# Moving column sums and a folding to other places in TensorE's queue, in a one-core convolution block

## The chip, the core and the metric

The kernel runs on one core of a Trainium2 chip. The metric is the device time of one execution in microseconds (us); lower is better. The engines are called as in the profile: PE (TensorE's matmuls), PEld (its weight loads), DVE (VectorE), ACT (ScalarE), POOL (GpSimd), SP (SyncE, which here issues nearly all DMAs). Each engine works through its own queue in order, and an instruction that must wait for another engine holds up everything behind it in its queue.

## The reference

One layer of a decoder with a convolution mixer, for 256 tokens of width 2048, all in float32. Cut to what is computed:

```python
mod = silu(c) @ mod_w + mod_b                 # 6 vectors of 2048: sh1, sc1, g1, sh2, sc2, g2
h = rms_norm(x, norm1_g) * (1 + sc1) + sh1
a, gt = split(h @ conv_w_in + conv_b_in)      # 2048 x 4096
u = a * sigmoid(gt)
u = depthwise_conv(u, 31 taps, causal) + dw_b # each of 2048 channels for itself
u = silu(layer_norm(u, ln_g, ln_b))           # mean and variance over the 2048 channels
x = x + (1 + g1) * (u @ conv_w_out + conv_b_out)
h = rms_norm(x, norm2_g) * (1 + sc2) + sh2
x = x + (1 + g2) * (square(relu(h @ mlp_w1)) @ mlp_w2)
```

## The kernel before

Channels lie on partitions: the width is cut into 16 tiles of 128 channels, each 128x256 (channels by tokens). A float32 product is made of reduced-precision parts: ACT writes the upper part `hi` of a weight tile (L209), DVE or POOL the rest `lo` (L213), and `mm` issues hi times hi, hi times lo and lo times hi.

The work on PE is a list of jobs, in order: 16 jobs "in" (job n gives tile n of `a` and of the gate), 8 jobs "out", and then the MLP's "up" and "down". The first eight "in" jobs are computed together at the start. The change lies in the jobs "in" 8 to 15, which stand between 136 and 291 us of the span. After the matmuls of job n (L238 and L239, for job 15 L234 to L236) its result is evacuated and gated: ACT L536, DVE L537, ACT L817 (sigmoid), DVE L819, which writes `u[n]`, the input of the convolution of tile n.

The convolution is shared out. Tiles 2, 3, 4, 5, 6, 8, 11 and 13 are done on DVE, one instruction per tap (L670, L672, L674, L676) and a joining sum (L679); `advance(n)` issues the next n of these steps, and the table `ADVANCE` says how many after each job. Tile 7 is shared by ACT and POOL. Tiles 0, 1, 9, 10, 12, 14 and 15 are done on PE (`pe_conv`, L802): `copy_wide` copies `u` into four shifted pieces (16 copies on ACT at L779, for tile 15 eight of them on DVE at L777), POOL writes the taps as diagonals (L787), and PE multiplies in strips of 32 columns. `CONV_AT` says after which job each such tile's convolution stands.

The layer norm needs sums of the convolved tiles and of their squares over all channels. For precision a shift is subtracted first: `find_shift` sums tiles 0 and 1 over their channels (two full-width matmuls, L428) into the PSUM tile `small`, and ACT writes the negative mean into the other half of `small` and into `shift` in SBUF (L737). From tile 8 on, DVE's second tap adds the shift from `small` (L674); `add_shift` (L741) and POOL (L908) add it to the others. `stats(b)` squares tiles 4b to 4b+3 on ACT (L480) and sums tiles and squares over channels with matmuls in strips of 32 columns (L747), again into `small`; `fold_stats` and `add_stats` finish.

The modulation vectors come in two ways. Rows (`mod_chunk`, L328) are matmuls in strips of 32 columns with weights that arrive by DMA, spread over the jobs; every 16 chunks, `mod_finish` folds the collected row into columns with small full-width matmuls (L375), from which DVE adds the bias (L366). Columns (`mod_col`, L408) are one DVE instruction of 128x2048 each; one of them is taken in job 15.

The order within each engine's queue is set by a planner that simulates the program when it is built. `tc.issue_after(x)` keeps what follows behind instruction x in that order, `urgent()` raises a priority; what has neither may be moved to where the planner sees room. The framework adds the waits that the data needs: a matmul that writes a tile waits for the engines that, by the order in which the code is written, read this tile before.

Two lines that the text below speaks of, the tap that reads `small` and the shift of tile 12 ahead of the column of job 15:

```python
            nc.vector.scalar_tensor_tensor(out, s, w, state["small"][:, T : 2 * T], op0=ALU.mult, op1=ALU.add)   # L674
                state["e_end"] = add_shift(cvs[3][:, 0:1, :], 1)                                                 # L915
        with tc.issue_after(state["e_end"]) if "e_end" in state else ExitStack():                                # L407
```

Of the kernel before, what the change touches and what calls it, by code (L numbers as in the profile page):

```python
# [11 lines left out]
ALU = mybir.AluOpType  # L12
# [5 lines left out]
KT = D // P  # L18
# [25 lines left out]
CONV_AT = {9: (0,), 10: (1,), 11: (9,), 12: (10,), 14: (12,), 15: (14,)}  # L44
POOL_TILE = 7
POOL_TAPS = {8: 2, 9: 7, 10: 7, 11: 7, 12: 7}
ADVANCE = {7: 41, 8: 10, 9: 44, 10: 47, 11: 39, 12: 34, 13: 24, 14: 99}
SHIFT = 2
COPY_AT = {8: 0, 9: 1, 10: 9, 11: 10, 13: 12}
PADDING = 752  # L50
UNSHIFTED = 7
# [17 lines left out]
def conv_block(ctx: ExitStack, tc: tile.TileContext, x, vec, dwq, c_row, mod_r, mod_c, w_first, w_in, w_out, w1, w2, out):  # L69
    nc = tc.nc  # L70
# [30 lines left out]
    ones = const.tile([P, P], F32, name="ones")  # L101
# [18 lines left out]
    state = {"used": 0}  # L120
# [247 lines left out]
    def mod_finish():  # L368
        while pending:
            ats, nj, r = pending.pop(0)  # L370
            n = len(ats)
            p = ps.tile([P, 512], F32, name="row", bufs=1)
            with urgent():
                for j in range(nj):
                    state["fold_end"] = nc.tensor.matmul(  # L375
                        p[:, n * j : n * j + n], r[:, j * P : (j + 1) * P], col("pick", 0, n), start=True, stop=True
                    )
                for b, at in enumerate(ats):
                    with tc.issue_after(state["lo_end"]) if "lo_end" in state else ExitStack():
                        mod_bias(at, nj, p[:, 0 : nj * n].rearrange("p (j n) -> p n j", n=n)[:, b, :])  # L380
# [16 lines left out]
    def mod_col(at, w=None):  # L397
        w = (take(("col", at)) if w is None else w).rearrange("p k n -> p (k n)")
        which, k = divmod(at, KT)
        acc = modc[:, at : at + 1]  # L400
        if which == SH2 and "cond" in state:
            n = HALF * P
            for half, total in zip(state["cond"], (acc, rest2[:, k : k + 1])):
                nc.vector.scalar_tensor_tensor(w[:, 0:n], w[:, 0:n], 1.0, half, op0=ALU.mult, op1=ALU.mult, accum_out=total)
                w = w[:, n:]
            return
        with tc.issue_after(state["e_end"]) if "e_end" in state else ExitStack():  # L407
            nc.vector.scalar_tensor_tensor(w, w, 1.0, cb, op0=ALU.mult, op1=ALU.mult, accum_out=acc)  # L408
        if which in amps:
            return nc.vector.scalar_tensor_tensor(  # L410
                amps[which][:, k : k + 1], acc, col("modb", at), col("n1g", k), op0=ALU.add, op1=ALU.mult
            )
        elif which != SH2:
            return mod_bias(at, 1, acc)
# [10 lines left out]

    def column_sum(p, tiles, first=True, last=True):
        for i, s in enumerate(tiles):
            nc.tensor.matmul(  # L428
                p, ones, s, start=first and i == 0, stop=last and i == len(tiles) - 1
            )  # L430

    def inverse_root(ms, src, scale, r, then=None):
        w = two()
# [109 lines left out]
    for k2 in range(HALF):  # L543
        s = two()
# [111 lines left out]
    def cv(k):  # L656
        return cvs[k // 4][:, k % 4, :]
# [73 lines left out]
    def find_shift():  # L731
        state["small"] = ps.tile([P, 512], F32, name="small", bufs=1)
        p = state["small"][:, 0:T]
        column_sum(p, [cv(k) for k in range(SHIFT)])
        state["shift"] = cp.tile([P, T], F32, name="shift", bufs=1)
        for dst in (state["small"][:, T : 2 * T], state["shift"]):
            nc.scalar.activation(dst, p, AF.Copy, scale=-1.0 / (SHIFT * P))  # L737

    def add_shift(tiles, n):
        by = state["small"][:, None, T : 2 * T].to_broadcast([P, n, T])  # L740
        return nc.vector.tensor_tensor(tiles, tiles, by, op=ALU.add).ins  # L741
# [9 lines left out]
    def stats(b):  # L751
        s = squares(cvs[b])
        for k in range(2):
            sum_round([(cv(4 * b + 2 * m + k), s[:, 2 * m + k, :]) for m in range(2)], b == 0 and k == 0)
# [15 lines left out]
    def copy_wide(ct, both=True):  # L770
        wides[ct] = cp.tile([P, 4, T + 28], F32, name="wide", bufs=2)
        for q in range(4):
            for g in range(4):
                dst = wides[ct][32 * q : 32 * q + 32, g, :]
                src = u[ct][32 * g : 32 * g + 32, q : q + T + 28]
                if both and g % 2:
                    nc.vector.tensor_copy(dst, src)  # L777
                else:
                    nc.scalar.activation(dst, src, AF.Copy)  # L779
# [14 lines left out]
    def pe_conv(ct, sq=None):  # L794
        wide = wides.pop(ct)
        diag = diags.pop(ct)
        p = ps.tile([P, 2, 2 * T], F32, name="mm", bufs=2)[:, 0, 0:T] if sq is None else ps_two()[:, 0, :]
        if sq is not None:
            nc.tensor.matmul(p, col("ident", 0, P), state["shift"], start=True, stop=False)
        for m in range(8):  # L800
            for g in range(4):
                state["conv_end"] = nc.tensor.matmul(  # L802
                    p[32 * g : 32 * g + 32, :], diag[:, 8 * g + m, :], wide[:, g, 4 * m : 4 * m + T],
                    start=(m == 0 and sq is None), stop=(m == 7),
                )
        with urgent():
            if ct == 14:
                nc.vector.scalar_tensor_tensor(cv(ct), p, col("dwb", ct), state["shift"], op0=ALU.add, op1=ALU.add)
            elif sq is None:
                nc.scalar.activation(cv(ct), p, AF.Identity, bias=col("dwb", ct))  # L810
            else:
                nc.vector.tensor_scalar(cv(ct), p, col("dwb", ct), None, op0=ALU.add)
                nc.scalar.activation(sq, p, AF.Square, bias=col("dwb", ct))
# [8 lines left out]
        return sg  # L822

    def mix(ct):
        pe_conv(ct)
        if ct == SHIFT - 1:
            find_shift()

    with urgent():
        split_w(jobs[HELD] + (0,), nc.gpsimd)  # L830
# [12 lines left out]
    for n, job in enumerate(jobs):  # L843
# [52 lines left out]
        else:  # L896
            for c in range(2):
                mm(p, c, job + (c,), hl, merged=kind == "out")
        mod_finish()
        if kind == "in":  # L900
            with urgent():
                gate(i, evac(p, out=p[:, :, 0:T]) if i < KT - 1 else p[:, :, 0:T])
# [9 lines left out]
            if n == KT - 2:  # L912
                add_shift(cvs[2][:, 1:3, :], 2)
            if n == KT - 1:
                state["e_end"] = add_shift(cvs[3][:, 0:1, :], 1)  # L915
                for key, w in taken:
                    mod_col(key[1], w)
            for ct in CONV_AT.get(n, ()):
                with tc.issue_after(state["mm_end"].ins):
                    mix(ct)  # L920
                with tc.issue_after(state["conv_end"].ins):
                    mods(rows)
                if rows:
                    state["rows_end"] = state["row_end"].ins
            if rows:
                mod_finish()
            with tc.issue_after(state["gated"]):
                advance(ADVANCE.get(n, 0))
            if n == KT - 2:
                with tc.issue_after(state["mm_end"].ins):  # L930
                    for b in range(2):
                        stats(b)
            if n < KT - 1:
                continue
            sq15 = two()
# [244 lines left out]
```

## Time and profile before

| what | us |
|---|---|
| median of 3 runs (1095.54 to 1095.91) | 1095.86 |
| the profiled execution | 1095.74 |
| its span | 1093.8 |
| PE busy in the span | 1075.9 (98%) |
| DVE busy | 748.5 (68%) |
| ACT busy | 520.1 (48%) |
| POOL busy | 217.4 (20%) |

In a row of a timeline stand the start, the length, the engine, the kernel's line, the operation, output and inputs with their shape, and how many instructions are merged in it; behind it in brackets how long the engine was idle before, and what ended that. One float32 matmul is two instructions of PE in the trace, so a group of 8 is 4 matmuls. In a table of windows, PEclk is the granted share of PE's clock.

### The profile page before, as it was taken

How to read it: one execution, taken by the hardware profiler on the slowest of the kernel's cores; microseconds unless marked ns; L12 is line 12 of the kernel's file. 1: busy time of each engine (PE TensorE's matmuls, PEld its weight loads, DVE VectorE, ACT ScalarE, POOL GpSimd, SP SyncE). 2: the span in 40 equal slices, each digit the busy share in tenths (PEclk: the TensorE clock that was granted, in tenths of full speed). 3: DMA queues.
4: the chain of work that ended last, by engine and by line, in shares of the span. 5: the costliest groups of instructions: out<-in, count | busy, mean ns of one | idle time of the engine just before them, and what ended most of it. 6: DMA issues, size and time to landing. Idle time of an engine off the chain costs nothing.

```text
span 1093.8 us, 15366 instructions
## 1 busy us (share of the span) xinstructions
PE 1075.9 (98%) x5970; PEld 889.9 (81%) x5970; DVE 748.5 (68%) x1019; ACT 520.1 (48%) x706; POOL 217.4 (20%) x149
## 2 busy tenths in 40 slices
PE   6999999999999999999999999999999999999998
PEld 3877876768699988888888888888888888888887
DVE  5777889997667877768855677545566665565653
ACT  4111398677675686444444444333444333444431
POOL 0000169989599251000000000000000000000000
PEclk8999999999999999999999999999999999999999
DMA  9999997995999967899977889657888877788611
GB/s 384 420 420 420 416 416 288 391 371 216 375 393 403 372 248 253 265 296 341 419 266 206 253 258 318 235 144 290 248 242 237 225 214 214 230 251 235 214 66 39
DMA packets 142314, 314.20 MB, mean 287 GB/s; under 512 B 87585, under 2 KB 105505, under 8 KB 107297
## 3 DMA queue, kind: packets, MB, share of 16 engines
q1 hardware_dynamic: 142096, 313.10, 81.6%
q8 instruction: 47, 0.77, 0.3%
q14 instruction: 25, 0.20, 0.0%
q10 hardware_dynamic: 146, 0.13, 0.0%
HBM read 301.13 MB, written 12.07 MB: 286 GB/s over the span
## 4 chain that ended last, share of the span: by engine, by line
PE 86%; DMA 10%; DVE 3%; ACT 1%; issue 0%; SPq 0%; ACTq 0%
PE mm L276 20%; PE mm L275 20%; PE mm L277 20%; DMA raw<-mod_c 9%; PE mm L238 6%; PE mm L239 3%; PE acc L235 2%; PE acc L234 2%; PE acc L236 2%; PE row L328 2%; PE mm L802 2%; DVE raw L408 1%; DMA x<-x 1%; DVE wide L777 1%; PE mm L234 0%; PE mm L236 0%
## 5 line engine op out<-in xcount | busy, mean ns | idle before, releaser
L209 ACT ACTIVATE hi<-raw 128x1024 fp32r<-128x1024 f32 x320 | 335.7, 1058 | 357.4 <-PE mm L277 328.3
L213 DVE TENSOR_TENSOR lo<-raw,hi 128x1024 fp32r<-128x1024 f32 x257 | 312.3, 1220 | 182.7 <-ACT hi L209 180.9
L276 PE MATMUL mm<-lo,u 128*128 128x512 f32 x496 | 193.0, 389 | 0.0
L275 PE MATMUL mm<-hi,u 128*128 128x512 f32 x496 | 193.0, 389 | 0.0
L277 PE MATMUL mm<-hi,u 128*128 128x512 f32 x496 | 192.9, 389 | 0.0
L277 PE MATMUL mm<-hi,hl 128*128 128x512 f32 x480 | 186.7, 389 | 0.0
L276 PE MATMUL mm<-lo,hl 128*128 128x512 f32 x480 | 186.7, 389 | 0.0
L275 PE MATMUL mm<-hi,hl 128*128 128x512 f32 x480 | 186.7, 389 | 0.0
L213 POOL TENSOR_TENSOR lo<-raw,hi 128x1024 fp32r<-128x1024 f32 x63 | 156.2, 2506 | 33.4 <-ACT hi L209 33.3
L408 DVE SCALAR_TENSOR_TENSOR raw<-raw,cond 128x2048 f32<-128x2048 f32 x50 | 117.8, 2358 | 40.5 <-DMA raw<-mod_c 40.5
L277 PEld LDWEIGHTS mm<-hi,u 128*128 128x128 f32 x496 | 93.1, 188 | 19.3
L276 PEld LDWEIGHTS mm<-lo,u 128*128 128x128 f32 x496 | 93.1, 188 | 19.1
L275 PEld LDWEIGHTS mm<-hi,u 128*128 128x128 f32 x496 | 93.1, 188 | 19.0
L277 PEld LDWEIGHTS mm<-hi,hl 128*128 128x128 f32 x480 | 90.1, 188 | 18.7
L275 PEld LDWEIGHTS mm<-hi,hl 128*128 128x128 f32 x480 | 90.1, 188 | 18.7
L276 PEld LDWEIGHTS mm<-lo,hl 128*128 128x128 f32 x480 | 90.1, 188 | 18.7
L676 DVE SCALAR_TENSOR_TENSOR acc<-u,v,acc 128x256 f32<-128x256 f32 x224 | 95.8, 488 | 1.8
L238 PE MATMUL mm<-hl,hi 128*128 128x512 f32 x224 | 80.3, 402 | 0.0
L580 PE MATMUL mm<-two,first 128*128 128x256 f32 x240 | 56.7, 390 | 8.9 <-ACT two L638 8.9
L234 PE MATMUL acc<-hl,hi 128*128 128x256 f32 x224 | 63.4, 283 | 0.0
L235 PE MATMUL acc<-hl,hi 128*128 128x256 f32 x224 | 63.4, 283 | 0.0
L236 PE MATMUL acc<-hl,lo 128*128 128x256 f32 x224 | 63.4, 283 | 0.0
(218 smaller groups left out, 1286.8 us busy)
## 6 DMA issues: line engine op xcount, KB each, us to landing
raw<-w SPq DMA_DIRECT2D x128, 1024.0 KB, 5.5
raw<-mod_c SPq DMA_DIRECT2D x62, 1024.0 KB, 11.3
raw<-mod_r SPq DMA_DIRECT2D x32, 1024.0 KB, 8.7
raw<-w_in SPq DMA_DIRECT2D x16, 1024.0 KB, 11.2
raw<-w_out SPq DMA_DIRECT2D x16, 1024.0 KB, 7.9
first<-w_first SPq DMA_DIRECT2D x15, 1024.0 KB, 19.8
flat<-two SPq DMA_DIRECT2D x30, 256.0 KB, 2.6
two<-flat SPq DMA_DIRECT2D x120, 64.0 KB, 4.4
```

The source lines that it names most:

```text
L209: state["w_hi"] = nc.scalar.activation(hi, w[:, ks, :], AF.Copy).ins
L213: end = by.tensor_tensor(lo, w[:, ks, :], hi.bitcast(F32), op=ALU.subtract)
L234: nc.tensor.matmul(out_p, w, m[:, 0:T], start=begin, stop=False)
L235: nc.tensor.matmul(out_p, w, m[:, T : 2 * T], start=False, stop=False)
L236: state["mm_end"] = nc.tensor.matmul(out_p, lo[:, k % HALF, :], m[:, 0:T], start=False, stop=end)
L238: nc.tensor.matmul(p[:, c, :], hi[:, k % HALF, :], m, start=(k == 0), stop=(k == KT - 1))
L275: nc.tensor.matmul(p, p_hi, hi, start=begin, stop=False)
L276: nc.tensor.matmul(p, p_hi, lo, start=False, stop=False)
L277: nc.tensor.matmul(p, p_lo, hi, start=False, stop=end)
L408: nc.vector.scalar_tensor_tensor(w, w, 1.0, cb, op0=ALU.mult, op1=ALU.mult, accum_out=acc)
L580: step = nc.tensor.matmul(held[n][:, c, :], w[:, 2 * n + c, :], h, start=k == 0 and c == 0, stop=k == KT - 1, skip_group_check=True)
L676: nc.vector.scalar_tensor_tensor(out, s, w, acc, op0=ALU.mult, op1=ALU.add)
```

## The change

- `find_shift` is issued ahead of the convolution of tile 9 (after job 11), and no longer behind that of tile 1 (after job 10). So that no tap reads the shift before it is there, `ADVANCE` gives job 10 five steps fewer and job 11 five more; five steps of job 13 go to job 14.
- `mod_finish`, the folding, is issued right behind the last matmul of its job, ahead of the convolution of that job; the later call behind the rows is dropped.
- `stats(0)` is issued in job 13 behind its rows, `stats(1)` in job 14 behind the convolution of tile 12; before, both were issued in job 14 behind its matmuls. The next job's matmuls are kept behind them.
- In job 15, the shift of tile 12 reads `shift` in SBUF, no longer `small`, and is written behind the column that job 15 takes, no longer ahead of it. `state["e_end"]` is set there, so that the column (L407) has no instruction to stand behind.
- The copies of tile 15 go ten to ACT and six to DVE, no longer eight and eight.

```diff
-ADVANCE = {7: 41, 8: 10, 9: 44, 10: 47, 11: 39, 12: 34, 13: 24, 14: 99}
+ADVANCE = {7: 41, 8: 10, 9: 44, 10: 42, 11: 44, 12: 34, 13: 19, 14: 99}
+SHIFT_AT = 9
...
     def find_shift():
...
-        column_sum(p, [cv(k) for k in range(SHIFT)])
+        end = column_sum(p, [cv(k) for k in range(SHIFT)])
...
+        return end
...
-                if both and g % 2:
+                if both and g % 2 and q:
                     nc.vector.tensor_copy(dst, src)
...
     def mix(ct):
-        pe_conv(ct)
-        if ct == SHIFT - 1:
-            find_shift()
+        with tc.issue_after(find_shift()) if ct == SHIFT_AT else ExitStack():
+            pe_conv(ct)
...
-        mod_finish()
+        with tc.issue_after(state["mm_end"].ins) if kind == "in" else ExitStack():
+            mod_finish()
...
             if n == KT - 1:
-                state["e_end"] = add_shift(cvs[3][:, 0:1, :], 1)
                 for key, w in taken:
                     mod_col(key[1], w)
+                state["e_end"] = nc.vector.tensor_tensor(cv(12), cv(12), state["shift"], op=ALU.add).ins
...
-            if rows:
-                mod_finish()
             with tc.issue_after(state["gated"]):
                 advance(ADVANCE.get(n, 0))
-            if n == KT - 2:
-                with tc.issue_after(state["mm_end"].ins):
-                    for b in range(2):
-                        stats(b)
+            if n in (KT - 3, KT - 2):
+                with tc.issue_after(state["row_end" if n == KT - 3 else "conv_end"].ins):
+                    stats(n - KT + 3)
+                state["rows_end"] = state["stats_end"].ins
```

More of the change, by code (lines that the diff above doesn't have):

```diff
@@ L427, in column_sum @@
         for i, s in enumerate(tiles):
-            nc.tensor.matmul(
-                p, ones, s, start=first and i == 0, stop=last and i == len(tiles) - 1
-            )
+            end = nc.tensor.matmul(p, ones, s, start=first and i == 0, stop=last and i == len(tiles) - 1).ins
+        return end
     def inverse_root(ms, src, scale, r, then=None):
@@ L737, in find_shift @@
             nc.scalar.activation(dst, p, AF.Copy, scale=-1.0 / (SHIFT * P))
+        return end
     def add_shift(tiles, n):
```

## The prediction

> **What bounds the kernel now.** I read the page first, then the windows, then the timelines of PE, DVE, ACT and POOL between 180 and 290 us.
>
> ```profile
> span 1093.8 us, 15366 instructions
> PE 1075.9 (98%) x5970; PEld 889.9 (81%) x5970; DVE 748.5 (68%) x1019; ACT 520.1 (48%) x706; POOL 217.4 (20%) x149
> 136.00:257.00 121.00, 121.00 (x982) 86.55 (x980) 113.52 (x274) 92.23 (x173) 106.29 (x69) 1.00 0.92 363
> ```
>
> PE is busy for 98% of the span. In the window of the "in" jobs (the last line; busy PE, PEld, DVE, ACT, POOL, then clock) it has no idle time at all, but DVE is busy for 113.5 of 121 us. So a microsecond saved on PE is a microsecond, and so is one in which PE has to wait for DVE, which has little room there. The change adds no instruction to PE: the order of the built program has the same matmuls in other places. What counts is the changes between strips and full width, and the waits.
>
> **Part by part. The first shift, and the folding.**
>
> ```profile
> 184.19 0.70 PE L428 MATMUL small<-cv,ones 128*128 128x256 f32 x2
> 184.82 3.64 PE L328 MATMUL row<-raw,cz 128*32 128x512 f32 x32
> 189.07 0.28 PE L239 MATMUL mm<-hl,lo 128*128 128x256 f32 x1
> 189.86 0.28 PE L239 MATMUL mm<-hl,lo 128*128 128x256 f32 x1
> 190.21 0.28 PE L239 MATMUL mm<-hl,lo 128*128 128x256 f32 x1
> 212.89 0.95 PE L375 MATMUL row<-v,rowsb 128*128 128x4 f32 x8
> 213.70 0.48 PE L238 MATMUL mm<-hl,hi 128*128 128x512 f32 x1
> 216.40 0.37 DVE L366 TENSOR_TENSOR modc<-row,v 128x4 f32<-128x4 f32 x4
> 223.37 0.70 DVE L537 TENSOR_TENSOR mm<-mm,two 128x512 f32<-128x512 f32 x1
> 223.95 3.62 PE L328 MATMUL row<-raw,cz 128*32 128x512 f32 x32
> ```
>
> The first column sum takes 0.63 (184.19 to 184.82) between two strip blocks, plus about 0.1 for leaving the strips, and the second 0.44 among full-width matmuls (L239 to L239 is 0.79 with the sum between, 0.35 without). Together 1.2. Side by side ahead of tile 9's strips I estimate two times 0.44: 0.3 gained. The folding costs 0.81 (212.89 to 213.70), and the same at its new place; 0.05 may be gained in the change to the strips behind it. The rows of job 12, at 223.95, now wait for DVE's four L366, which stand behind L537 of that job. Two taps of about 0.4 and L366's own 0.3 come later in their stead, so L537 starts 1.1 earlier, at 222.3, and L366 is done at 223.3, while PE gets there at 223.6: no cost, with 0.3 of cover; if the cover goes, the loss goes into the wait of the next part.
>
> **The sums of job 13 wait for DVE.** This is the term that decides. `stats(0)` writes `small`. In the code it stands behind `advance(19)` of job 13, and these steps contain the second tap of tile 13 (L674), which reads `small`. So the first of these matmuls waits for that tap, which needs `u[13]`, the gated result of job 13 itself. Before, they stood behind job 14, when the tap was long done.
>
> ```profile
> 239.00 1.92 PE L328 MATMUL row<-raw,cz 128*32 128x512 f32 x16
> 240.86 0.50 PE L238 MATMUL mm<-hl,hi 128*128 128x512 f32 x1
> 241.43 0.70 DVE L537 TENSOR_TENSOR mm<-mm,two 128x512 f32<-128x512 f32 x1 [0.42 <-ACT two L536]
> 242.68 0.48 DVE L819 SCALAR_TENSOR_TENSOR u<-mm,v,two 128x256 f32<-128x256 f32 x1 [0.55 <-ACT two L817]
> 244.31 0.48 DVE L674 SCALAR_TENSOR_TENSOR acc<-u,v,small 128x256 f32<-128x256 f32 x1
> ```
>
> The rows of job 13 end at about 240.8 now, 240.4 with the 0.35 gained; the tap starts at 244.31. DVE runs 0.6 ahead by then (L537's wait of 0.42 falls away, since ACT's copies and splits follow the earlier gate of job 12, and 0.2 comes from swapped taps): 243.7.
>
> And something gets in front of it. The column of job 15 (L408) had to stand behind tile 12's shift. That tie is gone, and in the planned order of the changed kernel the column stands between tile 11's last tap and L674. Its weights allow that: issued at 227.6, landed 13.4 later, at 241.0.
>
> ```profile
> DMA to landing us min/median/max: 13.4/13.4/13.4
> 266.39 0.42 DVE L741 TENSOR_TENSOR cv<-cv,small 128x256 f32<-128x256 f32 x1 [3.78 <-PE small L747]
> 266.73 3.52 DVE L408 SCALAR_TENSOR_TENSOR raw<-raw,cond 128x2048 f32<-128x2048 f32 x1
> L408 DVE SCALAR_TENSOR_TENSOR raw<-raw,cond x30: 2282/2288/2294, 12.4 to 120.5; 128x2048 f32<-128x2048 f32 x30
> 306.31 3.98 DVE L408 SCALAR_TENSOR_TENSOR raw<-raw,cond 128x2048 f32<-128x2048 f32 x1
> 243.30 1.92 POOL L787 TENSOR_TENSOR diag<-v,dwq_sb 128x1024 f32<-128x1024 f32 x1
> ```
>
> The column takes 2.29 while POOL is idle (the first 30), 3.52 and 3.98 beside POOL. At 243.7 POOL is in its diagonal, so I take 3.52 and keep 2.29 and 3.98 as ends. L674 then starts at 247.2 and ends at 247.7; PE goes on at 247.8. The stall is 247.8 - 240.4 = 7.4. The sums take 0.86 for a group of 16 (273.58 to 274.44, below) and 0.1 for going back to full width, so job 14 starts at 248.8 and not at 240.86: **+7.9**. Nothing refunds it: all later work of the "in" jobs hangs on PE's matmuls of job 14.
>
> Tile 12's shift (266.39) read `small` and waited 3.78 for the sums on it, with DVE idle; reading `shift` it needn't. PE waits for neither, so this is put at nothing, and the taps that job 13 leaves to job 14 fit into that idle time. SP's queue is the same; the buffer of the column is free some 20 earlier, so that the rows' weights come no later.
>
> By the rows the column might also wait for the whole of the diagonal and then run alone: the diagonal, 0.3 later than in its row, goes from 243.6 to 245.5, and with 2.29 behind it the column would take 4.1 and the time be 0.6 longer. The Trainium skill, page SBUF — State Buffer, section "SBUF: two separate sides", says just that: the pair of ports that DVE and GpSimd share is an exclusive lock, which the instruction that starts first holds to its end. The rows of 3.52 and 3.98 beside POOL agree in kind; which of the two comes first here hangs on 0.1 us, so I keep the row of 3.52.
>
> **PE's clock after the stall.**
>
> ```profile
> 19.46 0.80 PE L580 MATMUL mm<-two,first 128*128 128x256 f32 x1 [4.55 <-ACT two L638]
> 19.52:22.94 3.42, 3.42 (x8) 2.79 (x9) 3.38 (x5) 0.34 (x1) 0.00 (x0) 0.50 1.01 419
> 22.94:26.35 3.41, 3.41 (x17) 2.98 (x17) 1.25 (x4) 1.02 (x2) 0.00 (x0) 1.00 1.01 420
> ```
>
> The only long wait of PE behind the start, 4.55, is followed by 3.4 us at a granted clock of 0.50, with half as many matmuls (8 against 17 in equal windows). A wait of 7.4 should do the same, and half of 3.4 is lost: **+1.7**, with 0 and 2.6 as ends, because how long the low clock lasts may differ.
>
> **From tile 12's convolution to tile 15's.**
>
> ```profile
> 252.37 3.66 PE L802 MATMUL mm<-wide,diag 128*32 128x256 f32 x64
> 257.24 0.39 PE L234 MATMUL mm<-hl,hi 128*128 128x256 f32 x1
> 265.22 0.41 PE L747 MATMUL small<-sq,ones 128*32 128x256 f32 x2
> 266.20 0.39 PE L236 MATMUL mm<-hl,lo 128*128 128x256 f32 x1
> 270.11 3.66 PE L802 MATMUL mm<-wide,diag 128*32 128x256 f32 x64
> 273.58 0.39 PE L747 MATMUL small<-cv,ones 128*32 128x256 f32 x2
> 274.44 1.90 PE L328 MATMUL row<-raw,cz 128*32 128x512 f32 x16
> 276.90 0.62 PE L802 MATMUL acc<-wide,diag 128*32 128x256 f32 x2
> 278.79 3.76 PE L802 MATMUL acc<-wide,diag 128*32 128x256 f32 x61 [1.26 <-DVE wide L777]
> 265.69 11.62 POOL L213 TENSOR_TENSOR lo<-raw,hi 128x1024 fp32r<-128x1024 f32 x4 [2.59 <-ACT hi L209]
> 272.07 7.00 DVE L777 COPY wide<-u 32x284 f32<-32x284 f32 x8
> L777 DVE COPY wide<-u x8: 299/304/2411, 272.1 to 278.8; 32x284 f32<-32x284 f32 x8
> 272.07 3.61 ACT L779 ACTIVATE wide<-u 32x284 f32<-32x284 f32 x8 [0.55 <-DVE u L819]
> ```
>
> Before: 252.37 to 278.79, 26.4. After: tile 12's strips 3.5 (as 270.11 to 273.58), sums 0.97, job 15 without the break for sums 11.7 (its two pieces, 7.98 and 3.90, less 0.2 of changing), tile 14's strips 3.5, sums 0.86, then 2.46 as before (274.44 to 276.90): 22.9. There PE waits for the copies. Two of DVE's eight take 2.41, as long as an instruction of POOL, and the others 0.30: two lows of POOL still stand in the way, so that taking two copies from DVE saves 0.6, and POOL, which the column at 266.73 no longer delays, ends about 2.4 earlier relative to tile 12. The six end 23.6 behind tile 12's start; ACT's ten take 4.5 and are done earlier. A wait of 0.7 is left: 23.6 in all, **-2.8**.
>
> **Sum.** +7.9 + 1.7 - 2.8 = +6.8. The profiled execution took 1095.74 (span 1093.8 and 1.9 around it), 0.1 under the median, 1095.86. From it comes 1102.5, from the median 1102.7; I say 1102.6.
>
> **Rivals.** (1) PE's clock stays full: 1100.9. For it: only one such wait is in the trace, right after the start. The Trainium skill, page TensorE: Matmul & The Clock Gate, section "What's actually happening", speaks against it, with half rate after one idle window of about 3.4 us. (2) The column waits for the whole diagonal: 1103.2. (3) The column does not delay the tap, because it has run before: 1102.6 - 3.5 = 1099.1. Against it: the planned order, and the weights that land at 241.0. (4) The wait is longer, because the column's weights land late or the clock stays low for twice as long: 1104.3 to 1107. Against it: 2.7 between landing and use. (5) No wait: the tap is done when PE gets there. Then 0.35 is gained early, 0.9 paid for the sums in job 13 and 2.8 gained later: 1093.6, just faster. It decides if L674 ends by 240.4, 7.3 earlier than worked out; against it stands that `u[13]` is written only at 242.68.
>
> **How the numbers follow.** Forecast 0.45, rival 1 0.16, rival 2 0.20, rival 3 0.06, rival 4 0.08, rival 5 0.05. A measurement of this kernel can hardly tell less than 0.2% (2.2 us) from no change. The forecast's own range is 1100.8 to 1104.3: the column's ends, -1.2 and +0.5, 0.6 and 0.9 for the clock, 0.3 for the copies. Rivals 1 and 2 lie inside or near it; down to 1099.3 and up to 1105.0 it takes in the short column at full clock and the nearer half of rival 4. Rivals 1 to 4 are all slower by over 0.2%: 0.95, less 0.01 for their lower edges; rival 5 lies on the bound, so 0.03 same and 0.03 faster.
>
> **What would show it.** In the trace after, PE's rows of job 13 end near 240.4 and the first sum starts 6 to 8 later, released by DVE's L674, with the column ahead of it on DVE; a granted clock of 0.50 shows in the next window; the sums of squares no longer break job 15, and the wait for the last copies is under 1. I am wrong if PE has no wait near 240 to 248, or if the loss there is given back before tile 15.

## The result, and the profile after

The changed kernel takes 1102.42 us (median of 6 runs, 1101.24 to 1104.29) against 1095.81 (6 runs, 1095.54 to 1096.11): a ratio of 1.0061, with a 95% interval of 1.0048 to 1.0074. It is slower by 6.6, where 6.8 was forecast (1102.6). Its runs lie 3.05 apart, those of the kernel before 0.6. The profiled execution took 1101.44 (span 1099.3), 1.0 under the median and 5.7 over the profiled execution before. Most lines of the changed kernel are one higher than before: L329 are the rows, L409 the column, L748 the sums, L788 the diagonal, L803 PE's convolutions, L778 and L780 the last copies.

The view of waits on PE between 136 and 290, first of the kernel before and then of the changed one (total, times, longest):

```profile
PE acc L802 <- DVE wide L777: 1.3, 1, 1.3
```

```profile
PE small L748 <- DVE acc L674: 5.8, 1, 5.8
```

One wait has gone and another has come. The changed kernel's timelines of PE, DVE and POOL at that place, and where the loss ends:

```profile
238.68 1.93 PE L329 MATMUL row<-raw,cz 128*32 128x512 f32 x16
246.44 0.64 PE L748 MATMUL small<-cv,ones 128*32 128x256 f32 x2 [5.83 <-DVE acc L674]
248.30 0.80 PE L239 MATMUL mm<-hl,hi 128*128 128x512 f32 x1
260.50 3.66 PE L803 MATMUL mm<-wide,diag 128*32 128x256 f32 x64
291.49 5.36 PE L329 MATMUL row<-raw,cz 128*32 128x512 f32 x48
...
242.06 0.48 DVE L820 SCALAR_TENSOR_TENSOR u<-mm,v,two 128x256 f32<-128x256 f32 x1 [0.54 <-ACT two L818]
243.68 2.29 DVE L409 SCALAR_TENSOR_TENSOR raw<-raw,cond 128x2048 f32<-128x2048 f32 x1
245.89 0.49 DVE L674 SCALAR_TENSOR_TENSOR acc<-u,v,small 128x256 f32<-128x256 f32 x1
...
243.67 4.07 POOL L788 TENSOR_TENSOR diag<-v,dwq_sb 128x1024 f32<-128x1024 f32 x1
```

```profile
286.05 5.36 PE L328 MATMUL row<-raw,cz 128*32 128x512 f32 x48
```

PE ends the rows of job 13 at 240.6 and stands still until the tap L674 is done. On DVE this tap stands behind the gated product of job 13 and behind the column, as the prediction said. The column began within 0.01 of POOL's diagonal, and in this execution it was the diagonal that paid (4.07 for 1.93). The row in a fence of its own is PE's in the kernel before: the block of 48 rows that follows the "in" jobs starts at 286.05 there and at 291.49 here, 5.44 later, and the spans differ by 5.5. Nothing behind that block gives anything back.

The same stretch in windows (columns: length; busy PE, PEld, DVE, ACT, POOL with instructions; granted clock; share of the DMA engines; GB/s), cut where the granted clock changes:

```profile
240.06:243.47 3.41, 0.54 (x8) 0.00 (x0) 2.83 (x7) 0.91 (x2) 3.41 (x2) 1.00 0.97 344
243.47:246.88 3.41, 0.45 (x7) 0.22 (x11) 3.41 (x6) 0.00 (x0) 3.41 (x2) 0.50 0.98 401
246.88:250.29 3.41, 3.41 (x22) 2.08 (x15) 3.23 (x8) 1.06 (x1) 3.41 (x3) 0.50 1.01 423
250.29:253.70 3.41, 3.41 (x21) 2.98 (x20) 3.20 (x7) 1.06 (x1) 2.49 (x2) 1.00 1.11 394
```

A window in which PE did little is followed by one at half clock. PE came back at 246.44 and ran at half until 250.29, for 3.85. At half speed throughout that is a loss of 1.9; how much it really was is measured further down, by the kernels that keep a full clock.

### The profile page after: what moved, and what is told of

It is laid out like the page before. It is cut to its first block, busy times and chain, and to the rows that moved or that the text cites. A ratio compares the mean times of both kernels' runs of the same rounds, so it can differ in the third digit from the quotient of the medians.

```text
span 1099.3 us, 15368 instructions
## 1 busy us (share of the span) xinstructions
PE 1078.6 (98%) x5970; PEld 891.9 (81%) x5970; DVE 746.1 (68%) x1017; ACT 520.9 (47%) x708; POOL 217.4 (20%) x149
## 4 chain that ended last, share of the span: by engine, by line
PE 75%; DMA 11%; DVE 9%; ACT 4%; issue 1%; ACTq 0%; DVEq 0%; SPq 0%
PE mm L277 20%; PE mm L276 20%; PE mm L278 20%; DMA raw<-mod_c 7%; DVE acc L676 5%; PE acc L236 2%; PE acc L235 2%; PE acc L237 2%; PE mm L239 2%; DMA first<-w_first 2%; PE mm L240 1%; DVE raw L409 1%; ACT wide L780 1%; DMA raw<-w_in 1%; ACT hi L210 1%
## 5 line engine op out<-in xcount | busy, mean ns | idle before, releaser
L409 DVE SCALAR_TENSOR_TENSOR raw<-raw,cond 128x2048 f32<-128x2048 f32 x50 | 116.6, 2333 | 40.2 <-DMA raw<-mod_c 40.2
```

## Experiments

All were made after the prediction. Each is timed against the kernel before on the same chip, which took 1095.75 to 1095.80 there.

### Is it the wait for the tap? The sums written first

The sums write one half of `small`, and the tap reads the other half. So, if the prediction is right, the wait comes from the order in which the code is written and not from data, and it goes when the block stands ahead of `advance`:

```diff
+            if n in (KT - 3, KT - 2):
+                with tc.issue_after(state["row_end" if n == KT - 3 else "conv_end"].ins):
+                    stats(n - KT + 3)
+                state["rows_end"] = state["stats_end"].ins
             with tc.issue_after(state["gated"]):
                 advance(ADVANCE.get(n, 0))
-            if n in (KT - 3, KT - 2):
...
```

> The changed kernel, with the block of the sums written ahead of the steps that job 13 (and 14) advance. The matmuls of PE stand in the very same order; but the sums on small no longer come behind the second tap of tile 13 in the recorded program, so they don't wait for it. Theory: PE runs through from the rows of job 13 to job 14 with no wait, no lowered clock, and the time is that of the rival without a wait, about 1093.6 (bounds 1092.5 to 1095): 0.35 gained early, 0.9 paid for the sums in job 13, 2.8 gained behind it. Rival A (the places of the sums cost by themselves, by changing between strips and full width, and not by the wait): 1099 or more, with no wait in the trace. Rival B (the taps that now stand behind the sums delay DVE, which then delays the sigmoid products and the convolution of a later tile): a wait of PE of 1 to 4 behind DVE later in the job, 1095 to 1099.

Measured: 1093.69 (11 runs, 1093.46 to 1093.90), ratio 0.9980 (0.9971 to 0.9989). PE, DVE and POOL of this kernel:

```profile
238.60 1.92 PE L329 MATMUL row<-raw,cz 128*32 128x512 f32 x16
240.34 0.39 PE L748 MATMUL small<-cv,ones 128*32 128x256 f32 x2
241.31 0.49 PE L239 MATMUL mm<-hl,hi 128*128 128x512 f32 x1
276.61 1.27 PE L803 MATMUL acc<-wide,diag 128*32 128x256 f32 x15 [0.42 <-DVE wide L778]
...
264.00 1.80 DVE L918 TENSOR_TENSOR cv<-cv,shift 128x256 f32<-128x256 f32 x1 [2.12 <-ACT cv L811]
...
263.59 1.93 POOL L788 TENSOR_TENSOR diag<-v,dwq_sb 128x1024 f32<-128x1024 f32 x1
```

PE's matmuls stand in the same order as in the changed kernel, and there is no wait at 240 and no lowered clock. The whole loss of 8.7 between 1102.42 and 1093.69 is the wait and what hangs on it. The time is the one worked out for the rival without a wait. The tap L674 now stands behind the sums in the code, and that costs nothing: it starts at 245.80, behind the column as in the changed kernel, when PE has been at job 14 since 241.31.

### All but the sums

The changed kernel with the block of the sums as it was before (both behind the matmuls of job 14).

```diff
-            if n in (KT - 3, KT - 2):
-                with tc.issue_after(state["row_end" if n == KT - 3 else "conv_end"].ins):
-                    stats(n - KT + 3)
-                state["rows_end"] = state["stats_end"].ins
+            if n == KT - 2:
+                with tc.issue_after(state["mm_end"].ins):
+                    for b in range(2):
+                        stats(b)
```

> The changed kernel with the sums back in their old place (both behind job 14's matmuls); first shift, folding, columns, tile 12's shift by the shift tile and the last copies stay changed. Theory: no wait in job 13, 0.35 gained by shift and folding, and up to 0.6 by the last copies: about 1094.9 (1094.2 to 1095.5). Rival (another part of the change brings a loss of its own, say the untied column on DVE or the new place of the folding): 1097 or more, with the wait in another place.

Measured: 1093.60 (11 runs, 1093.37 to 1093.78), ratio 0.9978 (0.9969 to 0.9987). No other part brings a loss; in that the expectation was right. But the gain is 2.2 and not 0.9. Its PE and POOL:

```profile
276.60 1.28 PE L803 MATMUL acc<-wide,diag 128*32 128x256 f32 x19
...
265.72 9.52 POOL L214 TENSOR_TENSOR lo<-raw,hi 128x1024 fp32r<-128x1024 f32 x4
```

PE no longer waits at tile 15's convolution at all, though the sums of squares still stand where they stood. And with the sums moved as well and no wait, the time is the same (1093.69). The next three runs part the 2.2.

### The other parts, one by one, on the kernel before

The column of job 15 untied from tile 12's shift, and nothing else:

```diff
-                state["e_end"] = add_shift(cvs[3][:, 0:1, :], 1)
                 for key, w in taken:
                     mod_col(key[1], w)
+                state["e_end"] = nc.vector.tensor_tensor(cv(12), cv(12), state["shift"], op=ALU.add).ins
```

> The kernel before, with only the column of job 15 taken from behind tile 12's shift, and this shift by the shift tile. No sums are moved. Theory: DVE delays nothing that PE waits for in job 13; at the end of the in jobs POOL's lows are no longer held up by the column (11.62 for four in the kernel before, 9.5 without), so that DVE's and ACT's last copies end about 1 to 1.8 earlier, and the wait of 1.26 ahead of tile 15's convolution and what follows in it goes: about 1094.3 (1094.0 to 1095.0). Rival (the column is worth nothing by itself, the gain of 2.2 in e4 comes from the copies): 1095.5 to 1096.

The last copies ten to six, and nothing else:

```diff
-                if both and g % 2:
+                if both and g % 2 and q:
```

> The kernel before with only the last copies divided ten to six instead of eight to eight. Theory: two of DVE's copies still take 2.41 behind POOL, six end about 0.6 earlier than eight, so 0.6 of the wait of 1.26 goes and of what comes behind it: 1095.2 (1094.9 to 1095.4). Rival (the two that stand behind POOL are among the six and the rest is hidden): 1095.8. With the column alone (1094.37) and shift and folding alone the parts should add up to the 2.2 of the kernel with everything but the sums (1093.60): 1.4 + 0.35 + 0.4.

The first shift and the folding at their new places, with the steps of jobs 10 and 11 that belong to them, and nothing else:

```diff
-ADVANCE = {7: 41, 8: 10, 9: 44, 10: 47, 11: 39, 12: 34, 13: 24, 14: 99}
+ADVANCE = {7: 41, 8: 10, 9: 44, 10: 42, 11: 44, 12: 34, 13: 24, 14: 99}
+SHIFT_AT = 9
...
-        pe_conv(ct)
-        if ct == SHIFT - 1:
-            find_shift()
+        with tc.issue_after(find_shift()) if ct == SHIFT_AT else ExitStack():
+            pe_conv(ct)
...
-        mod_finish()
+        with tc.issue_after(state["mm_end"].ins) if kind == "in" else ExitStack():
+            mod_finish()
...
-            if rows:
-                mod_finish()
```

> The kernel before with the first shift ahead of tile 9's convolution and the folding behind the matmuls of its job (with the taps of jobs 10 and 11 as in the changed kernel), and nothing else. Theory: the 0.35 of the prediction's first step; in the profiled runs of the changed kernel and of the ones built on it job 13's rows start 0.3 to 0.4 earlier than before, and here too: 1095.4 (1095.2 to 1095.6). Rival (the gain is lost later, since the last copies wait for POOL and not for PE): 1095.8, no change.

| part alone | median (runs) | against before | ratio, 95% |
|---|---|---|---|
| column | 1094.37 (11) | -1.4 | 0.9987 (0.9978 to 0.9996) |
| copies | 1095.43 (11) | -0.3 | 0.9997 (0.9988 to 1.0006) |
| shift and folding | 1095.48 (11) | -0.3 | 0.9996 (0.9987 to 1.0005) |
| all but the sums | 1093.60 (11) | -2.2 | 0.9978 (0.9969 to 0.9987) |

The medians of the three add up to 2.0 of the 2.2. The column alone is told from no change by its interval; the other two are not. Shift and folding came out within the range given for them, the copies 0.03 above theirs. The column's gain is on POOL and DVE: in the kernel with the column alone, POOL's four lows take 9.51 (11.62 before), and the eight copies 5.43 (7.00 before).

```profile
265.85 9.51 POOL L213 TENSOR_TENSOR lo<-raw,hi 128x1024 fp32r<-128x1024 f32 x4 [0.77 <-ACT hi L209]
...
271.99 5.43 DVE L777 COPY wide<-u 32x284 f32<-32x284 f32 x8
```

With the copies alone six still take 6.35 behind the same lows, and half of PE's wait stays:

```profile
278.04 1.27 PE L802 MATMUL acc<-wide,diag 128*32 128x256 f32 x16 [0.62 <-DVE wide L777]
...
271.96 6.35 DVE L777 COPY wide<-u 32x284 f32<-32x284 f32 x6
```

### How much of the wait is the column? The sums alone, and the column late

Two runs: the kernel before with only the sums moved, as the changed kernel has them (the column still tied behind tile 12), and the changed kernel with the column tied behind the shift of tiles 9 and 10.

```diff
-            if n == KT - 2:
-                with tc.issue_after(state["mm_end"].ins):
-                    for b in range(2):
-                        stats(b)
+            if n in (KT - 3, KT - 2):
+                with tc.issue_after(state["row_end" if n == KT - 3 else "conv_end"].ins):
+                    stats(n - KT + 3)
+                state["rows_end"] = state["stats_end"].ins
```

> The kernel before, with only the sums moved (into job 13 behind its rows, and into job 14 behind its convolution), the column of job 15 still tied to tile 12's shift. Theory: PE waits for L674 without the column: L674 ends near 244.8 as before, PE is at the sums at 240.8, so a wait of about 4, plus 0.97 for the sums; job 14 starts near 245.8, +4.9. The clock falls to 0.50 for part of a window (1.4 to 1.7 lost). Behind it the sums of squares no longer break job 15, -2.2. Time about 1100 (1098.3 if the clock stays full). Rival (the sums alone cost nothing, and the whole loss is the column): 1094 to 1096. Rival (the sums alone bring the whole loss, the untied column nothing): 1102 or more.

```diff
             if n == KT - 2:
-                add_shift(cvs[2][:, 1:3, :], 2)
+                state["e_end"] = add_shift(cvs[2][:, 1:3, :], 2)
```

> The changed kernel, with the column of job 15 tied again behind a shift (the one of tiles 9 and 10, L742), so that on DVE it no longer stands ahead of L674. Nothing else moves. My theory (PE waits for DVE's L674, and the column is what stands in front of it): L674 starts near 243.7 instead of 245.9 (or instead of 247.7, where the column had to wait for POOL's diagonal), the wait of PE ahead of the first sum falls from 5.83 to about 3.6, and job 14 starts near 245.2. With half a clock window of 3.4 still at 0.50 (1.4 lost) that gives about 1099.4; with no lowered clock at all 1098.0. The rival that the column does not lengthen the wait (the sums wait for something else): 1101.5 to 1104, the wait still near 5.8 or longer. The rival that the column only moves its cost to a later place (the weights of rows come late): the wait is 3.6, but a new wait of 2 or more stands ahead of tile 15's rows, and the time is above 1101.

Measured: the sums alone 1100.30 (5 runs, 1099.80 to 1101.58), ratio 1.0044 (1.0032 to 1.0057); the column late 1098.66 (6 runs, 1097.42 to 1099.63), ratio 1.0026 (1.0015 to 1.0038). The sums alone, first PE's timeline and then windows, cut where the granted clock changes:

```profile
244.85 0.64 PE L747 MATMUL small<-cv,ones 128*32 128x256 f32 x2 [4.01 <-DVE acc L674]
```

```profile
240.70:244.11 3.41, 0.14 (x4) 0.00 (x0) 2.44 (x6) 1.19 (x3) 3.41 (x3) 1.00 0.89 348
244.11:247.53 3.42, 2.67 (x19) 1.31 (x20) 3.31 (x8) 0.59 (x1) 3.42 (x3) 0.50 0.91 343
247.53:250.94 3.41, 3.41 (x12) 2.93 (x12) 3.20 (x8) 0.46 (x1) 2.30 (x1) 0.50 1.01 423
```

The same two views of the column late:

```profile
244.03 0.41 PE L748 MATMUL small<-cv,ones 128*32 128x256 f32 x2 [3.58 <-DVE acc L674]
```

```profile
237.60:241.01 3.41, 2.85 (x22) 1.03 (x20) 3.22 (x7) 2.71 (x4) 3.41 (x2) 1.00 0.47 123
241.01:244.42 3.41, 0.39 (x8) 0.29 (x12) 2.87 (x8) 0.47 (x1) 3.41 (x3) 1.00 1.01 425
244.42:247.83 3.41, 3.41 (x23) 2.19 (x12) 3.30 (x6) 1.06 (x1) 3.41 (x3) 0.50 1.00 396
247.83:251.24 3.41, 3.41 (x22) 2.98 (x21) 3.34 (x5) 1.06 (x1) 3.41 (x1) 1.00 0.81 336
```

Both waits have the forecast length (about 4, and 3.6). So the tap alone makes a wait of 3.6 to 4.0, and the column in front of it adds 2.25 in the changed kernel (5.83 less 3.58), which is its own length. The median of the sums alone lies where I said. The execution that was profiled is the slowest of its five runs (1101.58), and in it the clock cost more than the 1.4 to 1.7 that I had put: PE worked at half from 244.85 to 250.94. The column late came out 0.7 under the 1099.4 that I gave for it, and above the 1098.0 for a full clock.

### Is the lowered clock a cost of its own? The wait filled with work

The kernel with the column late, and PE given matmuls that nobody reads, between the rows and the sums:

```diff
+            if n == KT - 3:
+                fill = ps.tile([P, 2, 2 * T], F32, name="mm", bufs=2)[:, 0, 0:T]
+                for _ in range(15):
+                    with tc.issue_after(state["row_end"].ins):
+                        state["row_end"] = nc.tensor.matmul(fill, ones, cv(0), start=True, stop=True)
```

> The kernel with the column tied late (e1), and in addition 15 matmuls whose result nobody reads (ones times tile 0's convolution, 128x256, about 0.22 each by the column sums of L429) put on PE between the rows of job 13 and the sums, so that they fill some 3.3 of the wait of 3.58. This is added work, none is left out. Theory (the idle time itself lowers the granted clock, and the lowered clock costs on top of the wait): job 14's matmuls start at about the same time as in e1 (up to 0.3 later), but run at clock 1.00, so the time falls by the 1.7 that e1's window at 0.50 cost: about 1097.0 to 1097.3, and the runs agree within 0.5 of each other. Rival (the clock falls for another reason, say DVE's or the DMA's load at this place): 1098.7 or more, with the window at 0.50 still there. Rival (the filling delays the sums): 1099 to 1101, the wait moved behind the filling.

Measured: 1100.45 (5 runs, 1100.31 to 1100.55), ratio 1.0042 (1.0028 to 1.0056). By its time this was a miss, in the range of the rival in which the filling delays the sums, and the mistake was mine: a float32 matmul of this size is two instructions and takes 0.44, so that the filling took 6.7 and held the sums up until 247.06. The clock stayed full, though, and the runs lie 0.24 apart. With 8 in place of 15:

> As the filled kernel (e5), with 8 matmuls instead of 15: one of them took 0.44 there (6.67 for 15) and not 0.22, so that the filling was twice as long as the wait and itself held the sums up by 2.5. Eight take 3.56 from 240.4, to 243.95, just inside the wait, which ends at 244.03. Added work, nothing left out. Theory (idle time lowers the clock): the first sum still near 244.0 to 244.1, no window at 0.50, the sums take 1.0 and job 14 11.51: about 0.54 and 0.81 less than in e1 (1.54 and 12.32), so 1097.3 (1097.0 to 1097.6), and the runs within 0.5 of each other. Rival (the clock falls also with a filled wait, and only e5's longer filling prevented it): 1098.6 to 1099.6, spread over 1 or more.

Measured: 1097.33 (11 runs, 1097.12 to 1097.80), ratio 1.0014 (1.0005 to 1.0023). First PE's timeline, then the window in which the column late had the half clock:

```profile
240.43 3.72 PE L932 MATMUL mm<-cv,ones 128*128 128x256 f32 x16
244.08 0.41 PE L748 MATMUL small<-cv,ones 128*32 128x256 f32 x2
```

```profile
244.00:247.40 3.40, 3.40 (x30) 2.46 (x30) 3.33 (x7) 1.06 (x1) 3.40 (x2) 1.00 1.00 402
```

The sums start where they started without the filling (244.08 for 244.03), and 3.6 more of work on PE makes the kernel 1.3 faster. The idle time is what lowers the clock, and the lowered clock is a cost on top of the wait. The runs of the two kernels overlap a little (1097.42 is the lowest with the column late, 1097.80 the highest with the filling), but the traces say the same. From the first sum to tile 12's convolution PE has the same matmuls in all of these kernels:

| kernel | first sum | tile 12's convolution | between | of this at 0.50 |
|---|---|---|---|---|
| sums written first | 240.34 | 252.61 | 12.27 | 0 |
| filled with eight | 244.08 | 256.58 | 12.50 | 0 |
| column late | 244.03 | 257.89 | 13.86 | 3.4 |
| changed kernel | 246.44 | 260.50 | 14.06 | 3.85 |
| diagonal first (next part) | 248.53 | 263.48 | 14.95 | 5.4 |
| sums alone | 244.85 | 259.94 | 15.09 | 6.1 |

Against the two kernels with a full clock, the lowered clock cost 1.4 to 1.6 with the column late, 1.6 to 1.8 in the changed kernel, 2.5 to 2.7 with the diagonal first and 2.6 to 2.8 with the sums alone: a little less than half of the time at 0.50. Why the two differ by 0.23 stays open.

### Column and diagonal: the diagonal first

In the changed kernel the two began at the same moment. Here the gated product of job 13 is written twice, which is work added to DVE ahead of the column:

```diff
-        state["gated"] = nc.vector.scalar_tensor_tensor(
-            u[i][:, PAD : PAD + T], t2[:, 0, :], col("b_in", i), sg, op0=ALU.add, op1=ALU.mult
-        ).ins
+        for _ in range(2 if i == 13 else 1):
+            state["gated"] = nc.vector.scalar_tensor_tensor(
+                u[i][:, PAD : PAD + T], t2[:, 0, :], col("b_in", i), sg, op0=ALU.add, op1=ALU.mult
+            ).ins
```

> The changed kernel, with job 13's gated product on DVE done twice (the same 128x256 result written again, about 0.4), so that the column comes up on DVE 0.4 after POOL has begun its diagonal instead of at the same moment. Theory A (the shared port is held by whichever instruction began first): the column takes as long as the rest of the diagonal and its own 2.29 together, 3.7 to 3.9; the first sum starts near 248.3, a wait of 7.7; with the lowered clock costing 1.7 to 3.4 the time is 1102.9 to 1104.8, median about 1103.7. Theory B (the two share the port in turns): the diagonal takes longer than its 1.93 and the column about 3.1; the first sum near 247.7, time 1102.2 to 1104. Rival (POOL's diagonal has no part in the column's time): column 2.29, the wait only 0.4 longer than in the changed kernel, 1101.6 to 1103.5. On the spread: if only the race for the port spreads the changed kernel's runs (3.05 between them), these runs agree within 0.5; if the place of the clock's windows does it, 1.7 of spread stays.

Measured: 1103.59 (5 runs, 1103.15 to 1104.33), ratio 1.0072 (1.0060 to 1.0085). The timelines of DVE, POOL and PE, and then the windows:

```profile
243.74 3.93 DVE L409 SCALAR_TENSOR_TENSOR raw<-raw,cond 128x2048 f32<-128x2048 f32 x1
...
243.62 1.90 POOL L788 TENSOR_TENSOR diag<-v,dwq_sb 128x1024 f32<-128x1024 f32 x1
...
248.53 0.64 PE L748 MATMUL small<-cv,ones 128*32 128x256 f32 x2 [8.00 <-DVE acc L674]
```

```profile
243.72:247.13 3.41, 0.00 (x0) 0.00 (x0) 3.41 (x2) 0.00 (x0) 3.41 (x2) 0.50 1.03 423
247.13:250.55 3.42, 2.02 (x17) 0.75 (x17) 3.31 (x9) 0.00 (x0) 3.42 (x2) 0.50 0.98 410
250.55:253.96 3.41, 3.41 (x11) 2.92 (x12) 3.23 (x8) 1.06 (x1) 1.68 (x1) 0.50 0.94 324
```

The diagonal took the lead by 0.12 and keeps its 1.90; the column takes 3.93: what was left of the diagonal (1.8, to 245.5) and nearly its own 2.29. In the changed kernel it was the other way round: the column 2.29, the diagonal 4.07; there the rows start within 0.01 of each other, which is too close to say who was first. The kernel with the sums written first shows the other order, with the column ahead by 0.06:

```profile
243.58 2.29 DVE L409 SCALAR_TENSOR_TENSOR raw<-raw,cond 128x2048 f32<-128x2048 f32 x1
...
243.64 4.00 POOL L788 TENSOR_TENSOR diag<-v,dwq_sb 128x1024 f32<-128x1024 f32 x1
```

So these two instructions do not take turns: whoever begins first goes through in its own time, and the other waits for all of it. The planner also put one tap behind the column, so the wait is 8.00 and not 7.7. The runs still lie 1.2 apart, with the race decided the same way by 0.12 at least in the execution that was profiled, which speaks against the race as the only source of the spread.

### A version that beats both

The sums written first, and the last copies twelve to four, since there PE waited for DVE's copies (to 276.9) while ACT's were done at 275.2:

```diff
-                if both and g % 2 and q:
+                if both and g % 2 and q > 1:
```

> The sums written first (e2), and of the sixteen last copies twelve on ACT and four on DVE instead of ten and six. In e2 PE waits for DVE's copies ahead of tile 15's convolution (0.42, and again between its matmuls; the convolution's 64 matmuls take 4.43 instead of 3.48), DVE's six end at 276.9 and ACT's ten at 275.25. Theory: two of DVE's four still stand behind POOL, so they end near 276.3, ACT's twelve near 276.15, and 0.4 of the wait goes: 1093.3 (1092.8 to 1093.5). Rival (ACT's copies now end last, or delay the squares behind them): 1093.7 to 1094.3.

Measured: 1092.99 (8 runs, 1092.86 to 1093.17), ratio 0.9974 (0.9964 to 0.9984): 2.8 faster than the kernel before and 9.4 faster than the changed one. Of the wait of 0.42, 0.17 is left, now for ACT:

```profile
275.88 0.59 PE L803 MATMUL acc<-wide,diag 128*32 128x256 f32 x3 [0.17 <-ACT wide L780]
```

## Why the prediction was right, and where its terms were off

**First shift and folding (0.35 gained, no wait).** Right. The rows of job 13 start 0.32 earlier in the changed kernel (238.68 for 239.00). The rows of job 12 start without a wait at 223.62, when DVE's L367 has been done for 0.2 (0.3 was forecast). Alone the part gives 0.3 by its median, which the interval does not tell from nothing.

**The wait of the sums of job 13 (7.4).** The mechanism was right in each link: L674 releases the first sum, the column stands in front of it, and both vanish when they are taken away (1098.66 without the column in front, 1093.69 without the wait). The size was off. In the profiled execution the wait is 5.83, mostly because the term "column beside POOL, 3.52" measured 2.29 there. 3.52 was a row of the right kind read in the wrong way. It fits, within 0.2, 2.29 and what was left of one of POOL's instructions (the column began at 266.73, 1.0 behind a low of about 2.4), and so here the length could only be 2.29 or about 4, by who began first. My rival 2 had the rule; I gave it 0.20 and took the middle.

**The clock (1.7, from 0 to 2.6).** Right that it falls, and it is a cost of its own (filled, 1.3 comes back). In the profiled execution it cost 1.6 to 1.8, as forecast. In the three other kernels with the wait it cost 1.4 to 2.8, so the upper end, 2.6, was just about reached. The forecast's range took only 0.6 off for this term, though its own lower end, 0, takes off 1.7; no run of the changed kernel came out under 1101.2.

**Tile 12's convolution to tile 15's (-2.8).** Right. To the block of 48 rows it is -2.7 (30.99, from 260.50 to 291.49, for 33.68 before, from 252.37 to 286.05). But the parts do not add up as the sum suggests. Without the sums moved, the untied column and the copies already bring 1.9 (31.77, from 252.06 to 283.83), because POOL's lows then end 2.1 earlier and PE's wait goes. And with the sums written first the stretch is 31.26, 0.3 longer than in the changed kernel: there PE waits 0.42 for the copies, and in the changed kernel the view of waits shows none. Moving the sums shortens PE's path behind tile 12, but what it wins goes into the sums in job 13 and into the wait for the copies: without the wait for the tap, the time is the same with the sums moved (1093.69) and without (1093.60), until the copies are divided anew.

**The sum.** For the profiled execution: -0.32, then from the rows of job 13 to tile 12's convolution 21.82 for 13.37, +8.45, then -2.69: +5.44 at the block of rows, against +6.8 forecast. Against the kernel with the sums first (14.01 over the same stretch) 7.81 of the 8.45 is wait and clock: the first sum starts 6.02 later behind the rows, and what follows takes 1.79 longer. The median of the runs is 1.0 above the profiled execution, and so comes out at the forecast 1102.6 within 0.2. That it is so close is partly luck: the column was put 1.2 too long for the execution that was profiled, and other executions lost about as much more.

**Why the runs lie apart.** This is argued and not shown, since only one execution of the changed kernel has a trace. Two things differ between the profiled executions of these kernels: which of column and diagonal goes first (1.6 between 2.29 and 3.93), and where the clock's windows fall (1.4 to 2.6 lost against the filled kernel). An estimate: put around the profiled execution's 1101.44, in which 1.6 was lost, they span 1101.2 to about 1104.1, as the runs do (1101.24 to 1104.29). The Trainium skill, page TensorE: Matmul & The Clock Gate, section "What's actually happening", says that the window of 3413 ns runs freely and does not start with the kernel; the windows above agree, with 3.41 and boundaries at 243.47, 244.42, 244.11 and 243.72. How often each happened in the runs that have no trace stays open; the mean granted clock of each run (0.994 to 0.997) does not follow their times.

## What to carry to other kernels

A write to one half of a tile can wait for a read of the other half: where a step is moved forward in a queue, look which accesses to the same tile are now written ahead of it, and move the step ahead of them too (here the same place in PE's queue cost 8.7 or nothing by the order of two blocks in the code). Price a wait on PE that is about as long as the clock's window (3.6 to 8.0 here, with windows of 3.4) with another 1.4 to 2.8 on top, and expect the runs to spread. And where DVE and POOL hold each other up as here, do not average the slow rows: take the instruction's own time, and add what is left of the other one's instruction if that began first.

## What the runs showed that was not expected

- PE does not come back to full clock with the first work. A window in which PE was busy for 2.67 of 3.42, at half clock, was still followed by one at 0.50 (the sums alone), and so was one with 2.02 (the diagonal first); after one with 2.85 of 3.41 at full clock the clock stayed at 1.00 (the column late). So where the wait ended inside a window that was already at 0.50 (the changed kernel, the sums alone, the diagonal first), PE was slowed for the rest of this window and for the next. Where it ended in a window still at 1.00 (the column late, at 244.03 of a window to 244.42), only the next one was slow. How much work keeps the clock up lies between these cases and is not shown.
- The shift of tile 12, which now reads `shift` in SBUF, took 1.80 in the kernel with the sums first, where it began 0.41 behind a diagonal of POOL, and 0.42 with the same shape from `small` before (266.39). In the changed kernel it reads `shift` too and takes 0.42, at 271.61, while POOL stands still. The Trainium skill, page SBUF — State Buffer, section "SBUF: two separate sides", says that an operation of DVE with two inputs from SBUF takes part in the lock; the row of 1.80 agrees, with 265.5 as the diagonal's end and 265.8 as its own. Here DVE had room, so it cost nothing.
- Work that nobody needs made the kernel faster by 1.3, since it kept the clock up.
